# Mixer C's heads emitted in two parts: the second head's projections and convolutions ahead of the first head's later steps

## The chip, the cores and the metric

One core of one Trainium2 chip runs the whole program. The metric is device time in microseconds, the median of three runs; less is better. Engines are named as in the profile: PE is TensorE, PEld its weight loads, DVE VectorE, ACT ScalarE, POOL GpSimd, SP the queue that issues most DMAs.

## What is computed

The reference is a trunk of two layers over 512 tokens of width 1024 in float32. Each layer is a mixer, then 16 experts with top-2 routing, then a gated input embedding. The change is in the second layer's mixer, where mixer C (a gated delta rule, four heads of width 128) and mixer D (forgetting attention, four heads) share one input and one output projection:

```python
def odd_mixer(hn, w_in, w_out, conv_c, a_log, dt_bias, norm_c, fd_bias):
    qc, kc, vc, gc, ac, bc, qd, kd, vd, fd = _split(hn @ w_in, ODD_SPLITS)
    qkv = jax.nn.silu(causal_conv(jnp.concatenate([qc, kc, vc], axis=-1), conv_c))
    ...
    qc = l2norm(_heads(qc, C_HEADS, HEAD_DIM))
    kc = l2norm(_heads(kc, C_HEADS, HEAD_DIM))
    ...
    oc = gated_deltanet(qc, kc, vc, ...)
    out_c = rmsnorm(oc, norm_c) * jax.nn.silu(_heads(gc, C_HEADS, HEAD_DIM))
    ...
    out_d = forgetting_attention(...)
    return jnp.concatenate([_merge(out_c), _merge(out_d)], axis=-1) @ w_out

def gated_deltanet(q, k, v, g, beta):      # per chunk of tokens
    ...
    sol = lax.linalg.triangular_solve(a, rhs, left_side=True, lower=True, unit_diagonal=True)
    ...
    def step(st, xs):                      # over the chunks, one after the other
        v_new = ui - jnp.einsum('bhlk,bhkv->bhlv', wi, st)
        o = jnp.einsum('bhlk,bhkv->bhlv', qdi, st) + jnp.einsum('bhls,bhsv->bhlv', qki, v_new)
        st = cdi[..., None, None] * st + jnp.einsum('bhsk,bhsv->bhkv', kdi, v_new)
        return st, o
```

## The kernel before

Products that need float32 precision are made of three fp32r matmuls (`mm3`, L235 to L237): every operand stands as a high part and a rest. Weights come from memory as 512 KB units, two to a load (`raw`), and `split` makes their two parts: a cast on ACT (L196, `whi`) and a difference on DVE (L197, `wlo`), each in a ring of four buffers. So the split of a unit waits until TensorE has read the unit four places ahead of it.

A head of mixer C is `mixer_c` (L766 to L886). Its **first part**, L767 to L773, makes four projections `proj_f` (q, k, v and the gate `gc`), each 24 matmuls of 512 columns into one PSUM buffer `m` of a pool of four, and a causal convolution with silu on three of them (`conv_silu`, L292 to L302): L294 on ACT evacuates, three L296 on DVE read the same PSUM buffer, L298 on POOL takes a maximum, L299 to L301 on ACT are the sigmoid, L302 on DVE multiplies. The gate is only copied (L773).

Its **later steps** are one chain. Two norms over q and k (`mean_ln`: L336 and L337 on ACT, L338 on DVE, L341 and L342 on TensorE, L344 on ACT), transposes (L795, L800, L815, L823), the inverse of the triangular matrix by six doublings (L828, L833 and the transposes of L837, with L829 and L834 on DVE and L838 on ACT between them), the last of them L842 and L843, the two right-hand sides (L845 to L854), then four chunks one after the other (L858 to L875): L866 makes the output of a chunk, L869 the update, L872 or L874 the new state on DVE, L863 and L864 the next correction. L877 to L886 norm the output, gate it (`e`, from L879 on POOL) and split it into `mixh` and `mixl` for the output projection (`out_proj`, L347).

The chunks here are 128 tokens long, four to the sequence. `mixer_d` (L888) is two projections, logits (L897 to L899), softmax, transposes (L377) and values (L385). `values` makes V for all four heads of mixer D: 96 matmuls into four PSUM buffers of the same pool.

The heads are emitted in the order of this table; tuples are output projections:

```python
ODD_ORDER = ["C0", "C1", "V", "D0", "C2", "D1", "C3", ("C0", "C1"), "D2", ("D0", "C2"), "D3", ("D1", "C3"), ("D2", "D3")]
```

In this stage no order is written out by hand. A scheduler that knows what each instruction waits for takes what is ready, and among that what was emitted first; so a head's chain comes interleaved with the projections that are emitted behind it. Each engine then runs its own list strictly in that order: an instruction that waits holds up all behind it on its engine. The tiles of C0 and C2 come from the ring `c0`, those of C1 and C3 from `c1`, all others of the stage from `w`.

Of the kernel before, what the change touches and what calls it, by code (L numbers as in the profile page):

```python
# [107 lines left out]
def tile_hybrid_trunk(ctx, tc, x, wst, gains, small, lam, rwt, cst, out, stop=None):  # L108
# [33 lines left out]
    class W:  # L142
        psum = turned = None
        banks = {}
        ring = ""
        pos = 0
        next = 0
# [21 lines left out]
    def pm(shape):  # L169
        return W.psum.tile(shape, F32, name="m", bufs=W.banks["m"])  # L170

    def pw(shape):
        n = W.ring if W.ring in W.banks else "w"
        return W.psum.tile(shape, F32, name=n, bufs=W.banks[n])
# [16 lines left out]
    def split(src, a=None, place=None):  # L191

        hi, lo = place or [wp.tile([128, 1024], F32R, name=n) for n in ("whi", "wlo")]
        if place:
            src = src.rearrange("p (k c) -> p k c", c=hi.shape[2])
        nc.scalar.copy(hi, src)  # L196
        nc.vector.tensor_sub(lo, src, hi.bitcast(F32))  # L197
        if a:
            return (hi.rearrange("p (a b) -> p a b", a=a), lo.rearrange("p (a b) -> p a b", a=a))
        return hi, lo  # L200

    def ahead(eng=None, pool=None):

        c = W.next
        if 2 * c >= len(UNITS):
            return
        W.loaded[c] = load(wst[c], eng, pool, c)
        W.next += 1
# [14 lines left out]
    def unit(kind, a=None, place=None):  # L223
        while UNITS[W.pos][0] == "pad":
            W.pos += 1
        assert UNITS[W.pos][0] == kind, (UNITS[W.pos], kind)
        c, half = divmod(W.pos, 2)
        if c not in W.loaded:
            W.next = c
            ahead()  # L230
        W.pos += 1
        return split(W.loaded[c][:, half, :], a, place=place)

    def mm3(ps, l, r, start, stop):
        mm(ps, l[0], r[0], start=start, stop=False)  # L235
        mm(ps, l[0], r[1], start=False, stop=False)  # L236
        mm(ps, l[1], r[0], start=False, stop=stop)  # L237
# [25 lines left out]
    def proj_f(w, parts=1):  # L263
        ps = pm([128, S])
        for i in range(parts):
            c = slice(i * S // parts, (i + 1) * S // parts)
            for k in range(KD):
                mm3(ps[:, c], (w[0][:, k, :], w[1][:, k, :]), (xt[0][:, k, c], xt[1][:, k, c]), k == 0, k == KD - 1)
        return ps
# [13 lines left out]
    def values(v):  # L283


        def emit(t, ps):
            for n in range(NH):
                nc.scalar.copy(v[n][:, t, :HD], ps[:, n * 128:(n + 1) * 128])

        proj_t(emit)  # L290
# [42 lines left out]
    def mean_ln(tmp, src, scale):  # L333

        sq, hi, lo = tmp(), tmp(F32R), tmp(F32R)
        act(sq, src, AF.Square)  # L336
        nc.scalar.copy(hi, sq)  # L337
        tt(lo, sq, hi.bitcast(F32), op=OP.subtract)  # L338
        ps = pw([128, S])
        one = oner.to_broadcast([128, 128])  # L340
        mm(ps, one, hi, start=True, stop=False)  # L341
        mm(ps, one, lo, start=False, stop=True)  # L342
        l = tmp()
        act(l, ps, AF.Ln, bias=epsc, scale=scale)  # L344
        return l

    def out_proj(mix, *halves):  # L347
        m = len(mix)
        for nh in halves or range(2):
            w = [unit("out", 2) for _ in range(m // 2)]  # L350
            for t in range(T):
                c = slice(t * 128, (t + 1) * 128)
                ps = pm([128, 512])
                for j in range(m):
                    x_, w_ = mix[j], w[j // 2]
                    mm3(ps, (x_[0][:, c], x_[1][:, c]), (w_[0][:, j % 2, :], w_[1][:, j % 2, :]), j == 0, j == m - 1)
                r = slice(nh * 512, (nh + 1) * 512)
                tt(h[:, t, r], h[:, t, r], ps, op=OP.add)
# [357 lines left out]
    def odd_mixer():  # L716
        with ExitStack() as cx:
# [46 lines left out]
            mix = {}  # L764

            def mixer_c(o_, n):  # L766
                q, k, v = tmp(), tmp(), tmp()  # L767
                pt = 1 if n else 2
                conv_silu(tmp, proj_f(unit("F", 8), pt), P_CC + 4 * n, q)
# [1 line left out]
                conv_silu(tmp, proj_f(unit("F", 8), pt), P_CC + 4 * (2 * NH + n), v)  # L771
                gc = tmp()
                nc.scalar.copy(gc, proj_f(unit("F", 8)))  # L773
                for src, sc in ((q, HD ** -0.5), (k, 1.0)):
                    l = mean_ln(tmp, src, 1.0)
                    act(l, l, AF.Exp, scale=-0.5)
                    stt(src, src, sc, l, op0=OP.mult, op1=OP.mult)
# [80 lines left out]
                o = pw([128, T, 128])  # L858
# [29 lines left out]
            def mixer_d(o_, n, vd):  # L888
                q, k = tmp(), tmp()
                act(q, proj_f(unit("F", 8)), AF.Copy, scale=HD ** -0.5)  # L890
                nc.scalar.copy(k, proj_f(unit("F", 8)))
                wt = [tmp() for _ in range(T)]

                def logits(i):
                    nk = 128 * (i + 1)
                    ps = pw([128, S])
                    mm(ps[:, :nk], q[:, i * 128:nk], k[:, :nk], start=True, stop=False)  # L897
                    mm(ps[:, :nk], sel[:, n:n + 1].to_broadcast([36, 128]), crs[:, :nk], start=False, stop=False)
                    mm(ps[:, nk - 128:nk], identb, maskq, start=False, stop=True)  # L899
                    return ps  # L900

                ps = logits(0)
                for i in range(T):
                    nk = 128 * (i + 1)
                    p, r = softmax_block(tmp(), ps, nk)
                    if i + 1 < T:
                        ps = logits(i + 1)
                    ts(p[:, :nk], p[:, :nk], r, None, op0=OP.mult)
                    put_Tj(wt, p, i)
                o = pv(vd[n], wt)  # L910
                mix[o_] = finish(xp, o, 5)

            vd = []
            for o in ODD_ORDER:
                W.ring = {"V": "v", "C0": "c0", "C1": "c1", "C2": "c0", "C3": "c1"}.get(o, "w")
                if o == "V":
                    vd = [q3(tmp()) for _ in range(NH)]
                    values(vd)
                elif isinstance(o, tuple):
                    out_proj([mix.pop(n) for n in o])  # L920
                elif o[0] == "C":
                    mixer_c(o, int(o[1]))
                else:
                    mixer_d(o, int(o[1]), vd)

# [575 lines left out]
    with ExitStack() as cx:  # L1501
        layer(0, cx)
        if stop == "ple0":
            return finish_h()
        odd_mixer()
# [124 lines left out]
```

## Time and profile before

| | us |
|---|---|
| median of three runs | 1477.32 (1477.06, 1477.32, 1483.2) |
| the profiled execution, its own time | 1478.86 |
| its span, first to last instruction | 1476.8 |
| TensorE busy | 1392.1 (94%) |
| DVE busy | 1123.4 (76%) |
| ACT busy | 928.6 (63%) |
| POOL busy | 132.4 (9%) |

All rows are of the profiled execution. The odd mixer begins near 699 us, when the last normed tile of the first layer is turned, and ends near 1056, with the last sum into `h`. Busy time of TensorE counts a matmul from its start to its modelled end, and these overlap: the distance from one start to the next tells the pace. The granted clock of the array is given as a share of full speed; it has two levels, 2.4 and 1.2 GHz.

### The profile page before, as it was taken

To read this page: it belongs to the slowest core of one execution; us is meant where nothing else is said; L and a number is where in the kernel's file an instruction comes from. 1 tells how busy PE (TensorE), PEld (TensorE's weight loads), DVE (VectorE), ACT (ScalarE), POOL (GpSimd) and SP (SyncE) were. 2 spreads that over 40 slices of the span, in tenths; PEclk is the share of its full clock that TensorE was granted. 3 is DMA by queue.
4 is the path that set the end of the run, shared out by engine and by line. 5 is a ranking of instruction groups with operands and counts; after the bars stand their busy time and mean duration, and the time that the engine had idled before them with its cause. 6 is when DMAs were issued, how large, how long until landed. Compare 5 with 4: busy or idle time off the path is not lost. (4 is left out here: it accounts for less than half of the span.)

```text
span 1476.8 us, 18718 instructions
## 1 busy us (share of the span) xinstructions
PE 1392.1 (94%) x6812; PEld 1104.7 (75%) x6812; DVE 1123.4 (76%) x1592; ACT 928.6 (63%) x1446; POOL 132.4 (9%) x140
## 2 busy tenths in 40 slices
PE   6999999969999999899989999999879999999796
PEld 4766777758888888667977878786668888888575
DVE  5488557689999999666874666665799999999665
ACT  4256554458888888657464464433458888888545
POOL 2010101010000000030110010000020000000030
PEclk9999999989999999999999999999989999999898
DMA  9223124779999998272411110115589999997261
GB/s 348 89 86 129 61 82 172 255 262 385 408 407 410 403 411 321 94 250 86 145 57 58 58 57 30 58 58 199 187 308 400 406 406 411 406 407 299 74 214 57
DMA packets 54938, 330.62 MB, mean 224 GB/s; under 512 B 6512, under 2 KB 6928, under 8 KB 22320
## 3 DMA queue, kind: packets, MB, share of 16 engines
q1 hardware_dynamic: 36576, 256.67, 44.6%
q0 software_dynamic: 12784, 52.69, 9.8%
q10 hardware_dynamic: 5472, 19.93, 3.4%
q8 instruction: 58, 0.95, 0.3%
q14 instruction: 48, 0.39, 0.1%
HBM read 299.37 MB, written 27.79 MB: 222 GB/s over the span
## 5 line engine op out<-in xcount | busy, mean ns | idle before, releaser
L1269 DVE TENSOR_TENSOR wlo<-raw,whi 128x1024 fp32r<-128x1024 f32 x392 | 456.6, 1219 | 13.8 <-ACT whi L1262 13.7
L1262 ACT CAST whi<-raw 128x1024 fp32r<-128x1024 f32 x392 | 396.0, 1055 | 50.5 <-PE m L237 36.7
L235 PE MATMUL m<-whi,eh 128*128 128x512 f32 x544 | 218.8, 402 | 0.0
L236 PE MATMUL m<-wlo,eh 128*128 128x512 f32 x544 | 215.5, 396 | 0.0
L237 PE MATMUL m<-whi,el 128*128 128x512 f32 x544 | 215.4, 396 | 0.0
L197 DVE TENSOR_TENSOR wlo<-raw,whi 128x1024 fp32r<-128x1024 f32 x110 | 133.3, 1225 | 69.8 <-ACT whi L196 69.5
L196 ACT CAST whi<-raw 128x1024 fp32r<-128x1024 f32 x110 | 113.9, 1050 | 64.6 <-PE m L237 33.3
L235 PE MATMUL m<-xth,whi 128*128 128x512 f32 (+1 forms) x368 | 142.2, 387 | 0.6 <-ACT xth L259 0.5
L237 PE MATMUL m<-xth,wlo 128*128 128x512 f32 (+1 forms) x368 | 141.5, 385 | 0.5 <-DVE wlo L197 0.5
L236 PE MATMUL m<-xtl,whi 128*128 128x512 f32 (+1 forms) x368 | 141.1, 384 | 0.8 <-DVE xtl L260 0.8
L235 PE MATMUL m<-whi,xth 128*128 128x512 f32 x288 | 118.9, 413 | 12.5 <-ACT xth L196 9.1
L237 PEld LDWEIGHTS m<-whi,el 128*128 128x128 f32 x544 | 102.4, 188 | 24.8 <-DVE exf L1112 0.4
L235 PEld LDWEIGHTS m<-whi,eh 128*128 128x128 f32 x544 | 102.7, 189 | 23.4 <-ACT eh L967 0.6
L236 PEld LDWEIGHTS m<-wlo,eh 128*128 128x128 f32 x544 | 102.7, 189 | 23.0
L237 PE MATMUL m<-whi,xtl 128*128 128x512 f32 x288 | 117.3, 408 | 0.5 <-DVE xtl L260 0.3
L236 PE MATMUL m<-wlo,xth 128*128 128x512 f32 x288 | 117.1, 406 | 0.5 <-DVE wlo L197 0.5
L235 PE MATMUL m<-whi,hh 128*128 128x512 f32 x272 | 112.1, 412 | 4.3 <-ACT whi L1262 4.3
L236 PE MATMUL m<-wlo,hh 128*128 128x512 f32 x272 | 109.3, 402 | 1.5 <-DVE wlo L1269 1.5
L237 PE MATMUL m<-whi,hl 128*128 128x512 f32 x272 | 108.8, 400 | 0.0
L237 PEld LDWEIGHTS m<-xth,wlo 128*128 128x128 f32 x368 | 69.7, 189 | 12.9 <-DVE wlo L197 1.0
L236 PEld LDWEIGHTS m<-xtl,whi 128*128 128x128 f32 x368 | 69.7, 189 | 12.5 <-DVE xtl L260 1.0
L235 PEld LDWEIGHTS m<-xth,whi 128*128 128x128 f32 x368 | 69.7, 190 | 12.4 <-ACT xth L259 0.9
(437 smaller groups left out, 2331.7 us busy)
## 6 DMA issues: line engine op xcount, KB each, us to landing
raw<-in_wst_dram SPq DMA_DIRECT2D x238, 1024.0 KB
raw<-in_wst_dram POOLq DMA_DIRECT2D x14, 1024.0 KB, 7.7
yrow<-gbc ACTq DMA_DIRECT2D x16, 512.0 KB
yrow<-y ACTq DMA_DIRECT2D x16, 512.0 KB
xrow<-raw POOLq DMA_DIRECT2D x8, 512.0 KB, 4.3
yrow<-tmp POOLq DMA_DIRECT2D x14, 256.0 KB, 9.5
h<-in_x_dram SPq DMA_DIRECT2D x4, 512.0 KB
raw<-in_wst_dram ACTq DMA_DIRECT2D x2, 1024.0 KB
```

What stands on the lines that cost most here:

```text
L196: nc.scalar.copy(hi, src)
L197: nc.vector.tensor_sub(lo, src, hi.bitcast(F32))
L235: mm(ps, l[0], r[0], start=start, stop=False)
L236: mm(ps, l[0], r[1], start=False, stop=False)
L237: mm(ps, l[1], r[0], start=False, stop=stop)
L1262: nc.scalar.copy(w[0], src)
L1269: nc.vector.tensor_sub(lo, src, hi.bitcast(F32))
```

## The change

`mixer_c` becomes a generator that stops once, behind its first part. For C1 the loop first begins the head (its projections and convolutions) and only then runs C0's later steps and C1's. C2 and C3 run as before, first part and later steps in one go. Nothing is computed otherwise.

```diff
             def mixer_c(o_, n):
+
                 q, k, v = tmp(), tmp(), tmp()
...
                 gc = tmp()
                 nc.scalar.copy(gc, proj_f(unit("F", 8)))
+                yield
                 for src, sc in ((q, HD ** -0.5), (k, 1.0)):
...
-            vd = []
+            vd, begun = [], {}
             for o in ODD_ORDER:
...
                 elif o[0] == "C":
-                    mixer_c(o, int(o[1]))
+                    begun[o] = mixer_c(o, int(o[1]))
+                    next(begun[o])
+
+                    for ring, c in {"C0": (), "C1": (("c0", "C0"), ("c1", "C1"))}.get(o, ((W.ring, o),)):
+                        W.ring = ring
+                        for _ in begun[c]:
+                            pass
```

What it does to the lists of the engines is shown at two places. In the changed program the line numbers from L774 on are one or two higher (L842 is L844, L848 is L850, L863 to L869 are L865 to L871).

**The first norms of C0**, on TensorE. Before, where `m_7889` is C1's k, `m_7929` C1's v, and `c0_7574` the cast square of C0's q:

```order
L237 MATMUL m_7889<-xth_6670,wlo_7886 128x512
L341 MATMUL w_7579<-c0_7574,oner_76 128x512
L235 MATMUL m_7929<-xth_6670,whi_7925 128x512
L236 MATMUL m_7929<-xtl_6671,whi_7925 128x512
L342 MATMUL w_7579<-c0_7575,oner_76 128x512
L237 MATMUL m_7929<-xth_6670,wlo_7926 128x512
```

Now, where `m_7705` is C1's gate, `m_8269` the first of V's four PSUM buffers and `c0_7732` the cast square of C0's q:

```order
L236 MATMUL m_7705<-xtl_6671,whi_7701 128x512
L237 MATMUL m_7705<-xth_6670,wlo_7702 128x512
L341 MATMUL w_7737<-c0_7732,oner_76 128x512
L342 MATMUL w_7737<-c0_7733,oner_76 128x512
L235 MATMUL m_8269<-whi_8273,xth_6670 128x512
```

and a little further on, where `m_8271` is V's third PSUM buffer and `c0_7745` the cast square of C0's k:

```order
L235 MATMUL m_8271<-whi_8273,xth_6670 128x512
L236 MATMUL m_8271<-wlo_8274,xth_6670 128x512
L237 MATMUL m_8271<-whi_8273,xtl_6671 128x512
L235 MATMUL m_8269<-whi_8303,xth_6670 128x512
L341 MATMUL w_7750<-c0_7745,oner_76 128x512
L312 MATMUL w_7757<-brs_7237,sel_75 128x512
L235 MATMUL m_8272<-whi_8273,xth_6670 128x512
L342 MATMUL w_7750<-c0_7746,oner_76 128x512
```

C0's norm of q has moved behind C1's v and gate, and its norm of k into the matmuls of V. On ACT, before, the cast of C0's k (`c0_7587`) stands ahead of the second exponent step of C1's q (`c1_7877`):

```order
L337 CAST c0_7574<-c0_7573 128x512
L196 CAST whi_8303<-raw_8301 128x1024
L299 ACTIVATE c1_7877<-c1_7877 128x512
L344 ACTIVATE c0_7582<-w_7579,epsc_67 128x512
L336 ACTIVATE c0_7586<-c0_7344 128x512
L776 ACTIVATE c0_7582<-c0_7582 128x512
L337 CAST c0_7587<-c0_7586 128x512
L300 ACTIVATE c1_7877<-c1_7877 128x512
```

Now it is `c0_7745`, and stands among the steps of C1's v (`c1_7692`, made from `c1_7687`):

```order
L294 ACTIVATE c1_7687<-m_7662,sm_65 128x512
L196 CAST whi_8361<-raw_8359 128x1024
L344 ACTIVATE c0_7740<-w_7737,epsc_67 128x512
L299 ACTIVATE c1_7692<-c1_7692 128x512
L778 ACTIVATE c0_7740<-c0_7740 128x512
L300 ACTIVATE c1_7692<-c1_7692 128x512
L336 ACTIVATE c0_7744<-c0_7344 128x512
L301 ACTIVATE c1_7692<-c1_7692 128x512
L337 CAST c0_7745<-c0_7744 128x512
L774 COPY c1_7698<-m_7705 128x512
```

It has moved behind the convolutions of C1's q, k and v.

**The last chain, C3's**, on TensorE from its right-hand sides on. Before, where `m_9832` and `m_9864` are D3's projections:

```order
L848 MATMUL w_9470<-c1_9329,c1_9468 128x128 x4
L853 MATMUL w_9477<-c1_9353,c1_9322 128x128 x4
L866 MATMUL w_9485<-c1_9303,c1_9466 128x128
L235 MATMUL m_9832<-xth_6670,whi_9828 128x512
L236 MATMUL m_9832<-xtl_6671,whi_9828 128x512
L237 MATMUL m_9832<-xth_6670,wlo_9829 128x512
L869 MATMUL w_9487<-c1_9466,c1_9483 128x128
```

Now, where `m_9979` belongs to the output projection of D1 and C3, its part for D1:

```order
L237 MATMUL m_9979<-whi_9967,mixl_9109 128x512
L850 MATMUL w_9470<-c1_9329,c1_9468 128x128 x4
L855 MATMUL w_9477<-c1_9353,c1_9322 128x128 x4
L868 MATMUL w_9485<-c1_9303,c1_9466 128x128
L871 MATMUL w_9487<-c1_9466,c1_9483 128x128
L865 MATMUL w_9491<-state_9489,c1_9467 128x128
L867 MATMUL w_9485<-c1_9304,state_9489 128x128
L868 MATMUL w_9485<-c1_9303,c1_9466 128x128
L871 MATMUL w_9496<-c1_9466,c1_9483 128x128
```

The chunk steps now follow each other with nothing between; D3's projections have all moved ahead of them. On DVE at the same place, now:

```order
L845 TENSOR_TENSOR c1_9353<-c1_9353,w_9460 128x512
L197 TENSOR_TENSOR wlo_10080<-raw_10077,whi_10079 128x1024
L847 TENSOR_TENSOR c1_9468<-c1_9353,betc_7235 128x512
L852 TENSOR_TENSOR c1_9353<-c1_9353,ktc_7236 128x512
L858 TENSOR_TENSOR c1_9483<-c1_9322,dc_9298 128x512
```

Before, L843 (now L845) and L845 (now L847) stood side by side; the last weight split of the stage has moved between them.

## Rows read from the trace of the kernel before

**Rows 1.** The page: the span, and the busy time of each engine with its share of the span and its instructions.
```profile
span 1476.8 us, 18718 instructions
PE 1392.1 (94%) x6812; PEld 1104.7 (75%) x6812; DVE 1123.4 (76%) x1592; ACT 928.6 (63%) x1446; POOL 132.4 (9%) x140
```

**Rows 2.** Busy time by stretch of the span: the stretch, its length, busy us and instructions of PE, PEld, DVE, ACT and POOL, the granted clock, the DMA engines' share and GB/s.
```profile
700.00:750.00 50.00, 44.78 (x289) 40.01 (x290) 39.73 (x57) 27.22 (x47) 8.90 (x5) 0.98 0.38 128
740.00:750.00 10.00, 5.35 (x21) 3.98 (x20) 7.60 (x11) 6.09 (x10) 3.82 (x2) 0.92 0.32 106
750.00:800.00 50.00, 49.41 (x293) 40.73 (x292) 29.90 (x53) 23.36 (x39) 2.98 (x2) 0.98 0.12 43
1000.00:1050.00 50.00, 48.38 (x222) 34.34 (x222) 25.44 (x53) 17.80 (x51) 3.65 (x5) 0.97 0.49 192
```

**Rows 3.** What TensorE waited for between 690 and 1040 us: who, whom, us in total, times, the longest.
```profile
PE w L341 <- ACT c L337: 4.6, 1, 4.6
...
PE w L377 <- DVE w L908: 1.6, 1, 1.6
```

**Rows 4.** TensorE in order of time around the wait in front: start, duration, line, output and inputs, and in brackets the idle time before it and what ended it.
```profile
743.16 0.40 PE L236 MATMUL m<-xtl,whi 128*128 128x512 f32 x1
743.39 0.39 PE L237 MATMUL m<-xth,wlo 128*128 128x512 f32 x1
748.43 0.80 PE L341 MATMUL w<-c,oner 128*128 128x512 f32 x1 [4.65 <-ACT c L337]
749.02 0.63 PE L235 MATMUL m<-xth,whi 128*128 128x512 f32 x1
749.45 0.63 PE L236 MATMUL m<-xtl,whi 128*128 128x512 f32 x1
...
753.79 0.40 PE L341 MATMUL w<-c,oner 128*128 128x512 f32 x1
...
758.38 0.60 PE L795 MATMUL w<-cs,c 128*128 128x128 f32 x4
```

**Rows 5.** ACT in order of time in the same place: the first sigmoid steps of C0's k and v, the copy of C0's gate and the cast of C0's q.
```profile
737.35 0.63 ACT L299 ACTIVATE c<-c 128x512 f32<-128x512 f32 x1 [3.90 <-POOL c L298]
...
744.77 0.63 ACT L299 ACTIVATE c<-c 128x512 f32<-128x512 f32 x1 [3.36 <-POOL c L298]
...
746.63 0.57 ACT L773 COPY c<-m 128x512 f32<-128x512 f32 x1
...
747.76 0.62 ACT L337 CAST c<-c 128x512 fp32r<-128x512 f32 x1
```

**Rows 6.** DVE in order of time in the same place: the three L296 of C0's v and a weight split.
```profile
739.95 2.31 DVE L296 SCALAR_TENSOR_TENSOR c<-m,sm,c 128x511 f32<-128x511 f32 x3
742.17 1.22 DVE L197 TENSOR_TENSOR wlo<-raw,whi 128x1024 fp32r<-128x1024 f32 x1
```

**Rows 7.** POOL in order of time: the maxima of C0's k and v and of C1's q, and L879 of C0.
```profile
734.99 2.33 POOL L298 TENSOR_SCALAR c<-c 128x512 f32<-128x512 f32 x1 [5.17 <-DVE c L296]
742.40 2.33 POOL L298 TENSOR_SCALAR c<-c 128x512 f32<-128x512 f32 x1 [5.09 <-ACT c L294]
748.26 1.49 POOL L298 TENSOR_SCALAR c<-c 128x512 f32<-128x512 f32 x1 [3.52 <-DVE c L296]
...
803.25 1.72 POOL L879 TENSOR_SCALAR c<-c 128x512 f32<-128x512 f32 x1 [28.41 <-PE w L869]
```

**Rows 8.** TensorE in order of time at the end of the stage, from L842 of C3 to the output projection of D1 and C3; the matmul at 1021.25 is the first that reads C3's result.
```profile
997.29 1.13 PE L842 MATMUL w<-c,c 128*128 128x128 f32 x8
...
1000.08 1.13 PE L848 MATMUL w<-c,c 128*128 128x128 f32 x8
...
1001.94 0.43 PE L866 MATMUL w<-c,c 128*128 128x128 f32 x2
...
1002.91 0.38 PE L869 MATMUL w<-c,c 128*128 128x128 f32 x2
...
1003.84 0.40 PE L863 MATMUL w<-state,c 128*128 128x128 f32 x2
...
1004.75 0.38 PE L866 MATMUL w<-c,c 128*128 128x128 f32 x2
1004.97 0.39 PE L869 MATMUL w<-c,c 128*128 128x128 f32 x2
...
1009.68 0.38 PE L866 MATMUL w<-c,c 128*128 128x128 f32 x2
...
1019.58 0.41 PE L377 MATMUL w<-cs,w 128*128 128x128 f32 x2 [1.57 <-DVE w L908]
...
1021.25 0.58 PE L235 MATMUL m<-whi,mixh 128*128 128x512 f32 x1
1021.62 0.63 PE L236 MATMUL m<-wlo,mixh 128*128 128x512 f32 x1
1022.05 0.63 PE L237 MATMUL m<-whi,mixl 128*128 128x512 f32 x1
```

**Rows 9.** DVE in order of time in the same place.
```profile
1003.34 0.29 DVE L874 COPY state<-w 128x128 f32<-128x128 f32 x1 [2.07 <-PE w L869]
1004.27 0.29 DVE L864 TENSOR_TENSOR c<-c,w 128x128 f32<-128x128 f32 x1 [0.64 <-PE w L863]
...
1016.16 1.23 DVE L197 TENSOR_TENSOR wlo<-raw,whi 128x1024 fp32r<-128x1024 f32 x1 [0.53 <-ACT whi L196]
```

**Rows 10.** ACT in the same place: the cast of the stage's last weight unit.
```profile
1015.09 1.05 ACT L196 CAST whi<-raw 128x1024 fp32r<-128x1024 f32 x1 [0.17 <-PE m L236]
```

## Prediction

> **What bounds the kernel now.** I read the page's busy shares first, then the busy time by stretch, then the list of who TensorE waits for, then the order of time on the four engines at two places. The page says TensorE works for 94% of the span [rows 1]. In the odd mixer, where the change is, the stretches say the same more sharply: 49.41 of 50 us at 750 to 800, against 44.78 at 700 to 750 and 48.38 at 1000 to 1050 [rows 2]. So the stage is a queue of TensorE work with few holes, and a change of order can only fill holes or make new ones. What can be filled is small: the list of waits has one of 4.6 us on the ACT cast of L337 and one of 1.6 us on the DVE scaling of L908 [rows 3], and the rest sums to less than these. Each hole costs a little more than itself, because the array comes back at half pace: main matmuls start every 0.23 us before the large wait and every 0.43 us after it [rows 4], and the matmul durations stretch to 0.63 us after the small one too [rows 8]. The granted clock is 0.92 at 740 to 750, and 0.97 over the last 50 us [rows 2].
>
> **What the order says.** All work is the same; 16 projections, 4 chains of head steps and the fillers between them stand in another order. I call a 512-column matmul of a projection a main matmul. In front, between the wait and the first transposes of C0 (L795), TensorE had 29 main matmuls before and has 81 now: all of C1's v and gate, then 33 of V. At the end, between L842 of C3 and the first matmul that reads C3's result (an output projection), it had 46 main matmuls before and has 7 now. Everything between is the same chain on other cover, with four to seven main matmuls behind each step as before; I cost it at nothing, and the cover is V and D0's q and k for C0, C2's projections for C1, and so on. POOL's and SP's queues hold the same instructions, POOL with C1's three maxima (L298) ahead of C0's L879, before which POOL stood idle for 28.41 us anyway [rows 7], and with four weight loads ahead of C3's L879; these wait for D3's last projection, which now ends before C3's steps do. I cost both at nothing.
>
> **The front.** The wait of 4.65 us goes: C1's v and gate need no result that is late (their weights were split, and their PSUM buffers come free with L296 of C0's v at 739.95 + 2.31 [rows 6] and the copy L773 at 746.63 + 0.57 [rows 5]). What is late next are the convolutions. ACT, DVE and POOL work on one convolution at a time: ACT's L299 of C0's k, at 737.35, and of v, at 744.77, are 7.42 us apart [rows 5], since the next evacuation L294 stands behind L301 in ACT's queue; inside lie 2.31 us of L296 on DVE [rows 6] and 2.33 us on POOL [rows 7]. A projection on TensorE takes 24 x 0.23 = 5.5 us. With six convolutions in a row TensorE gains 1.9 us on each and runs out of the four PSUM buffers. The POOL maximum of C1's q starts at 748.26 and takes 1.49 [rows 7]; nothing ahead of it has moved, so C1's q has its L299 at 749.8, k at 757.2, v at 764.6. C1's v gives its PSUM buffer back when POOL can start on it, at about 764.6 - 2.33 - 0.1 = 762.1. TensorE reaches the V matmuls that need this buffer (m_8271) at 743.6 + 48 x 0.23 + 0.7 for L341 and L342 + 12 x 0.23 = 758.1: **a new wait of 4 us**. The next one is L341 of C0's k. Its cast L337 stood ahead of C1's L300 on ACT and stands now behind C1's v, the sixth ACT instruction from 764.6; at a pitch of 0.6 (L773 to L337 is two in 1.13) it starts 3.0 later, and with its 0.62 [rows 5] it ends at 768.2, while TensorE is there at 762.1 + 7 x 0.23 = 763.7: **another 4.5 us**. From L341 of k to L795 it took 758.38 - 753.79 = 4.6 [rows 4], so L795 comes at 772.8, 14.4 later than before, with 52 more main matmuls done (52 x 0.23 = 12.0). The front loses 2.4 us instead of gaining 6.
>
> What the trace does not show is POOL's time for C1's k and v. The rows have 2.33 where DVE's split (L197) starts just ahead of it, as at 742.17 and 742.40 [rows 6, 7], and 1.49 elsewhere. The new order puts a split behind both, so I take 2.33; at 1.49 twice the front loses 0.7. The upper bound is the slow pace after both waits: the first wait cost some 7 matmuls x 0.2 = 1.4 us on top [rows 4], so +3.8. The Trainium skill ("SBUF — State Buffer", section "Who interferes with whom") holds that VectorE and GpSimd take one shared port pair as an exclusive lock, so that the later one blocks fully. Here the split would hold POOL until 743.39, which makes 0.99 + 1.49 = 2.48 where the row has 2.33; for the two together the lock would add 0.3 us to the front's loss, and no lock would take off 1.7. The measured 2.33 decides; it lies near the lock.
>
> **The end.** The chain of C3 took 1021.25 - 997.29 = 23.96 us from L842 to the first matmul on its result [rows 8]; the cover is now gone, so I add the chain up. L842 to L848 is 2.79 [rows 8]; a weight split stands now between L843 and L845 on DVE, 1.2 us more (1.22 for one [rows 6]): 4.0. L848 to the first L866 is 1.9 [rows 8]. Then three chunk updates: L869 to DVE's copy 0.43 and 0.29 for it, L863 to L864 0.43 and 0.29 again [rows 8, 9], two hand-overs of 0.1 (DVE's end at 1003.63 to L863 at 1003.84 is the upper bound of one) and 0.2 from L866 to L869 [rows 8], 1.9 each, 5.6 in all, where they took 1009.68 - 1001.94 = 7.74 between main matmuls [rows 8]. From the last L866 to the output projection it was 11.57 [rows 8]; the weight split that lay in it, L196 on ACT ahead of L883 and L197 on DVE ahead of L884 [rows 9, 10], is gone, about 1.0, so 10.6. Sum 22.1 us. TensorE's own load in it falls by 39 x 0.23 = 9.0 and gains 0.3 of transposes. Had the old order lost nothing more, 23.96 - 9.0 + 0.3 = 15.3 would do; **the end loses 22.1 - 15.3 = 6.8 us**, as waits of L848, of the nine update matmuls and of the output projection. Bounds: without the split in the way and with 1.5 us saved by an emptier DVE, +4; with the array at half pace through the stretch (a matmul takes 0.63 us for 0.40 then [rows 4, 8], and some 13 of them stand one behind the other in this chain), 3 us more, +10. I take the sum, because its durations are of the same instructions.
>
> **Sum.** +2.4 + 6.8 = +9.2 us. The profiled execution took 1478.86 us, of which 1476.8 is span; it would become 1488.1. It is 1.5 above the median of the three runs, 1477.32, so I forecast 1486.5. What follows the stage (routing, experts) starts from the end of the odd mixer and is passed on unchanged.
>
> **Rivals.**
> - *The front pays.* If the convolutions keep TensorE's pace once no head steps lie between them, the wait of 4.65 and 1.4 of slow pace go, -6; with the end's +6.8 that is 1478. For it: DVE is busy for 29.90 and ACT for 23.36 of the 50 us from 750 [rows 2]. Against it: the 7.42 us were measured where no head steps lay between. Chance 0.20.
> - *Slow clock.* The end is idle for 6.8 of 22.1 us in pieces of 1 to 2 us. One piece of 1.57 was followed by a slow stretch at 1021 [rows 8]. With 3 us more at the end, by the bound above, and 1.4 behind each of the front's waits it is +6: 1492.5. Against it: at 1002 to 1009 the steps ran at full pace. Chance 0.14.
> - *Faster.* C3's chain is shorter than I add up, because nothing else stands in DVE's and ACT's queues. It decides at 15.3 us from L842 to the output projection: below, the end costs nothing and its old wait (1.57, and 1.5 of slow pace) goes too. With the front's -6 that makes 1468. Against it: 2.79 + 1.9 + 10.6 is 15.3 already, without one chunk update. Chance 0.05.
> - *Forecast*, both waits: 0.61.
>
> **How the numbers follow.** About 0.5% (7.4 us) is what a measurement of this kernel can tell from no change. Slower by more: four fifths of the forecast's cases (its own range is 1482 to 1491, and a fifth of it lies under 1484.7) and the slow clock, 0.62. Faster: 0.05. The rest, 0.33. The range reaches from the first rival to above the second, 1478 to 1494, and leaves out the faster one and the thin ends.
>
> **What would show it.** Right: L341's wait on C0's q gone; a TensorE wait of 3 to 4 us of a V matmul on DVE's L296 and one as long of L341 on ACT's L337, both at 758 to 769; L795 near 773; L842 of C3 to the output projection 21 to 23 us with holes at L848 and between the chunk updates; the stage ending some 9 us later. Wrong in front: L795 before 769. Wrong at the end: less than 17 us, or other main matmuls between the updates than the order shows.

## The result

The changed kernel takes 1496.97 us (1496.71 to 1499.27, four runs) against 1479.08 (1477.06 to 1483.2, four runs) for the kernel before on the same chip: a ratio of 1.0124, 95% interval 1.0111 to 1.0137. It is **slower by 17.9 us**; the forecast was 9.2 slower, and the range ended 3 us below the result. The direction and both places were right, the sizes were not.

From here on, L797 of the changed kernel is L795 of before, L844 is L842, and so on (two lines more from L775).

The page of the changed kernel, first lines, and its busy time by stretch (columns as in [rows 2]):

```profile
span 1494.9 us, 18719 instructions
PE 1401.2 (94%) x6812; PEld 1109.9 (74%) x6812; DVE 1125.9 (75%) x1592; ACT 928.8 (62%) x1446; POOL 132.2 (9%) x140
```
```profile
700.00:750.00 50.00, 48.18 (x305) 43.28 (x306) 41.13 (x59) 28.62 (x50) 6.58 (x4) 0.97 0.37 128
740.00:750.00 10.00, 10.00 (x45) 8.06 (x44) 6.52 (x9) 6.59 (x12) 2.33 (x1) 1.00 0.29 105
750.00:800.00 50.00, 44.57 (x228) 35.47 (x227) 27.83 (x46) 24.20 (x42) 6.14 (x3) 0.93 0.12 43
1000.00:1050.00 50.00, 43.04 (x213) 30.30 (x212) 21.92 (x44) 15.82 (x38) 3.63 (x5) 0.86 0.37 147
```

The hole of 740 to 750 is gone. Against [rows 2], TensorE's busy time falls from 49.41 to 44.57 at 750 to 800 and from 48.38 to 43.04 at 1000 to 1050, and the granted clock with it. The same is in the list of who TensorE waits for in the changed kernel, from 690 to 1110 (in all, times, longest):

```profile
PE w L341 <- ACT c L337: 5.1, 2, 3.8
...
PE w L377 <- DVE w L910: 2.2, 2, 1.2
...
PE m L235 <- DVE c L296: 1.7, 1, 1.7
...
PE w L839 <- DVE c L836: 1.1, 2, 0.6
PE w L850 <- DVE c L847: 1.1, 1, 1.1
```

**Where the 18 us lie.** The first main matmul of C0's q and the last matmul of the last output projection bound the stage, before and now:

```profile
698.72 0.62 PE L235 MATMUL m<-xth,whi 128*128 128x256 f32 x3 [0.46 <-ACT xth L259]
...
1054.61 0.39 PE L237 MATMUL m<-whi,mixl 128*128 128x512 f32 x1
```
```profile
701.65 0.62 PE L235 MATMUL m<-xth,whi 128*128 128x256 f32 x3 [0.46 <-ACT xth L259]
...
1073.37 0.40 PE L237 MATMUL m<-whi,mixl 128*128 128x512 f32 x1
```

The stage takes 371.7 us instead of 355.9: **15.8 of the 18.1 us** between the two spans. 2.9 arose ahead of it and 0.6 was given back behind it, in parts that the change does not touch. Ten of the eleven kernels below start the stage between 699.1 and 700.6 (the other one alters the stages ahead), so part of that 2.9 is how two executions differ; the rest was not followed.

To see where inside the stage, I take an account of TensorE: each of its instructions at a fixed weight (0.233 us for 512 columns of a main matmul, 0.12 for 256, 0.15 for a step of 128, 0.2 to 0.235 for longer ones), summed in program order. The sum is 302.6 us for every kernel here. What a stretch took beyond its sum is called lost in it. Example: before, the first transposes come 758.38 - 698.72 = 59.7 us into the stage with 50.8 of work ahead of them: 8.9 lost. "Left" is the main matmuls, at full pace, behind C3's last doubling (L842 before).

The weights of the steps are low: the four products of L842 take 0.88 us at full clock (997.29 to 998.17), 0.22 each. With the distances of the full-pace rows instead, the work is 326.8 us, and before has 10.1, 12.7 and 6.2 lost, the change 13.8, 14.5 and 16.6. So much of a column, the middle one above all, is work and not loss; the differences between kernels are what the table tells, and those come out the same (3.7, 1.8 and 10.4).

| kernel | time | ahead of C0's first transposes | up to C3's last doubling | from there to the end | left |
|---|---|---|---|---|---|
| before | 1479 | 8.9 | 31.8 | 12.6 | 31.6 |
| change | 1497.0 | 12.5 | 33.6 | 23.0 | 22.6 |
| e1_yield_k | 1479.2 | 9.1 | 32.4 | 11.2 | 31.6 |
| e2_yield_v | 1488.0 | 10.7 | 32.9 | 18.0 | 26.3 |
| e3_fill_end | 1491.9 | 12.5 | 33.6 | 9.9, fillers counted as work | 22.6 + 11.2 |
| e4_five_banks | 1503.2 | 12.4 | 32.8 | 21.6 | 22.6 |
| e5_pair_steps | 1482.8 | 12.6 | 34.5 | 9.5 | 37.2 |
| e6_both_pairs | 1486.0 | 16.2 | 29.4 | 16.2, a longer stretch | 56.5 |
| e7_max_on_dve | 1483.1 | 4.0 | 29.3 | 21.7 | 22.6 |
| e8_before_max_on_dve | 1478.4 | 4.1 | 28.5 | 19.2 | 26.3 |
| e9_norm_first | 1492.5 | 7.6 | 32.1 | 23.3 | 23.0 |
| e10_pair_and_max | 1468.3 | 4.3 | 28.8 | 10.2 | 33.5 |
| e11_pairs_and_max | 1466.3 | 4.2 | 23.3 | 14.5, a longer stretch | 56.5 |

The change costs 3.6 us in front (forecast 2.4), 1.8 between (forecast nothing) and 10.4 at the end (forecast 6.8). Each line is one execution, and two executions differ: behind L842 e1 has TensorE's order of before, instruction by instruction, and loses 11.2 there for 12.6. One difference in front is not the order's either. In the changed kernel and in nine of the eleven others TensorE runs at half pace for some 3 us near 725 (granted clock 0.57 at 724 to 728 in the changed kernel, 1.00 at 722 to 726 before) and loses 1.5, in projections ahead of all that the change moves; the executions of before, e4 and e6 do not have it there. Where TensorE waits further on in the front, it comes to that wait later and waits less; where no wait is left (e7, e8, e10, e11), the 1.5 is part of the 4.0 to 4.3.

**The front, as forecast.** TensorE and ACT of the changed kernel in order of time:

```profile
764.38 0.47 PE L235 MATMUL m<-whi,xth 128*128 128x512 f32 x1 [1.67 <-DVE c L296]
...
765.86 0.40 PE L235 MATMUL m<-whi,xth 128*128 128x512 f32 x1
770.02 0.79 PE L341 MATMUL w<-c,oner 128*128 128x512 f32 x1 [3.76 <-ACT c L337]
...
771.46 0.79 PE L235 MATMUL m<-whi,xth 128*128 128x512 f32 x1
...
777.00 0.60 PE L797 MATMUL w<-cs,c 128*128 128x128 f32 x4
```
```profile
751.89 0.63 ACT L299 ACTIVATE c<-c 128x512 f32<-128x512 f32 x1 [0.45 <-POOL c L298]
...
759.33 0.63 ACT L299 ACTIVATE c<-c 128x512 f32<-128x512 f32 x1 [3.95 <-POOL c L298]
...
766.75 0.63 ACT L299 ACTIVATE c<-c 128x512 f32<-128x512 f32 x1 [3.37 <-POOL c L298]
...
769.36 0.60 ACT L337 CAST c<-c 128x512 fp32r<-128x512 f32 x1
```

C1's three L299 stand 7.44 and 7.42 us apart, the cycle that the forecast took from C0's [rows 5]. Both waits are there: V's matmul for its PSUM buffer, 1.7 us (forecast 4; 1.5 of the difference is the half pace near 725, by which TensorE came later), and L341 for the cast L337, 3.8 (forecast 4.5). Behind the second main matmuls have 0.63 to 0.79 us and start every 0.43 for 4 us, which I had left to the upper bound; behind the first they keep full pace.

**The end.** TensorE from C3's last doubling to the first matmul that reads C3's result:

```profile
1014.67 1.13 PE L844 MATMUL w<-c,c 128*128 128x128 f32 x8
1018.49 1.13 PE L850 MATMUL w<-c,c 128*128 128x128 f32 x8 [1.05 <-DVE c L847]
...
1020.34 0.43 PE L868 MATMUL w<-c,c 128*128 128x128 f32 x2
...
1026.36 0.49 PE L868 MATMUL w<-c,c 128*128 128x128 f32 x2 [0.16 <-DVE c L866]
1028.18 0.69 PE L341 MATMUL w<-c,oner 128*128 128x512 f32 x1 [1.33 <-ACT c L337]
...
1033.28 1.49 PE L899 MATMUL w<-w 128*128 128x384 f32 x2
...
1036.80 0.66 PE L377 MATMUL w<-cs,w 128*128 128x128 f32 x2 [1.20 <-DVE w L910]
...
1040.40 0.78 PE L235 MATMUL m<-whi,mixh 128*128 128x512 f32 x1
```

From L844 it is 3.8, 1.9, 6.0 and 14.0 us to these marks; forecast 4.0, 1.9, 5.6 and 10.6. Only the last is off. The granted clock by stretch, in the changed kernel:

```profile
1020.00:1025.00 5.00, 3.77 (x25) 2.89 (x23) 1.22 (x4) 0.82 (x2) 0.00 (x0) 1.00 1.01 426
1025.00:1030.00 5.00, 3.07 (x13) 2.20 (x13) 1.37 (x4) 1.21 (x2) 1.48 (x1) 0.83 1.00 424
1030.00:1035.00 5.00, 4.00 (x9) 1.77 (x8) 1.63 (x5) 3.43 (x9) 0.00 (x0) 0.50 0.64 269
1035.00:1040.00 5.00, 3.80 (x9) 1.40 (x9) 2.92 (x7) 1.51 (x5) 0.00 (x0) 0.50 0.00 0
```

At 1030 to 1040 TensorE runs at 0.50, that is 1.2 GHz, and what it runs there is D3: logits (L899 to L901) and transposes (L377). The two last heads share every queue. ACT and DVE show how D3's pace becomes C3's:

```profile
1034.14 0.63 ACT L885 ACTIVATE c<-c 128x512 f32<-128x512 f32 x1
```
```profile
1035.63 0.56 DVE L363 TENSOR_REDUCE nm<-w 128x1 f32<-128x384 f32 x1 [2.14 <-PE w L901]
...
1036.57 0.75 DVE L886 SCALAR_TENSOR_TENSOR c<-w,sm,c 128x512 f32<-128x512 f32 x1
```

C3's L886 reads what L885 made by 1034.77, but stands in DVE's queue behind D3's row maximum, which waited 2.14 us for logits that TensorE made at half pace, and starts at 1036.57.

### The profile page after: what moved, and what is told of

Its sections match the earlier page's. It is cut to its first block, busy times and chain, and to the rows that moved or that the text cites. A ratio compares the mean times of both kernels' runs of the same rounds, so it can differ in the third digit from the quotient of the medians.

```text
span 1494.9 us, 18719 instructions
## 1 busy us (share of the span) xinstructions
PE 1401.2 (94%) x6812; PEld 1109.9 (74%) x6812; DVE 1125.9 (75%) x1592; ACT 928.8 (62%) x1446; POOL 132.2 (9%) x140
## 5 line engine op out<-in xcount | busy, mean ns | idle before, releaser
L196 ACT CAST whi<-raw 128x1024 fp32r<-128x1024 f32 x110 | 114.1, 1050 | 69.3 <-PE m L237 33.3
L237 PEld LDWEIGHTS m<-xth,wlo 128*128 128x128 f32 x368 | 70.3, 191 | 12.5 <-DVE wlo L197 1.0
```

## The experiments

Theory A: the chains of the four heads stand one behind the other, and every us of projections that runs ahead of the first is cover that the last one lacks; its holes then also bring the clock down. Rival B: the waits in front are the loss. Rival C: at the end it is the chain's latency alone, not the clock.

**Dose.** The second head stops earlier.

```diff
                 conv_silu(... P_CC + 4 * (NH + n), k)
+                if n == 1:
+                    yield
...
-                yield
+                if n != 1:
+                    yield
```

> The second head stops after its k convolution; its v and gate are emitted behind the first head's later steps. In the order of the instructions TensorE then has main matmuls worth 48.3 us at full pace ahead of the first head's first transposes (46.4 before the change, 58.5 with it), and from the first head's L842 on the order is that of the kernel before. Theory A, borrowed cover (each us of matmuls put ahead of the first head's chain is missing under the last head's chain): 1477 to 1480, the end of the stage as before (24 us from the third line of the update chain, L842, to the first output projection on the last head's result), a wait of 2 to 3 us left in front. Rival B, the early start itself disturbs the front (convolutions and head steps in each other's way): 1482 to 1486, with new waits at the first head's norms.

Measured: 1479.23 us, ratio 0.9999 (0.9988 to 1.0010). The order behind the last head is that of before, and its loss, 11.2 us, is near that of before (12.6). In front the wait of L341 on L337 is 3.4 us (4.6 before; TensorE came to it 1.5 later, by the half pace near 725), and 0.2 us more is lost than before.

The same with the two lines behind v's convolution:

> The second head stops after its v convolution; only its gate is emitted behind the first head's later steps. Main matmuls ahead of the first head's transposes: 53.2 us (46.4 before, 58.5 with the whole change). Main matmuls left behind the last head's L842: 26.3 us (31.6 before, 22.6 with the change). Theory A, borrowed cover: about 0.55 of the loss of the whole change, 1487 to 1490. Rival B, the loss is that of the six convolutions in a row in front and of the waits they cause: nearly the whole loss, 1494 to 1497.

Measured: 1487.99 us, ratio 1.0061 (1.0041 to 1.0080), half of the loss, as A had it and B had not: the front lost 1.8 us more than before, the end 5.4.

**Fillers at the end**, behind D3 in the changed kernel:

```diff
+                if o == "D3":
+                    for i in range(48):
+                        ps = pm([128, S])
+                        mm(ps, xt[0][:, i % KD, :128], xt[0][:, i % KD, :], start=True, stop=True)
```

> The whole change, and 48 matmuls of 512 columns that nobody reads (11.2 us at full pace) at the lowest place in the order, which puts 11 behind L844 of the last head, 2 to 3 between its chunk updates, 6 behind the last update and 13 between the last softmax head's steps. They do no useful work; they only fill holes. Theory A with the clock (the holes let the array fall to half pace, and the last heads' steps at half pace are part of the loss): granted clock 1.0 from 1015 to 1045, L844 to the output projection 21 to 23 us instead of 25.7, the time 2 to 4 us shorter, 1493 to 1495. Rival C, the chain's latency alone is the loss: no gain, or up to 2 us more where a filler stands in the way, 1497 to 1499.

Measured: 1491.94 us (1491.47 to 1493.87), 5.0 less than the changed kernel and 1 below what A with the clock expected, with 11 us more on TensorE. Its stretches:

```profile
1025.00:1030.00 5.00, 5.00 (x26) 3.51 (x24) 1.46 (x4) 1.72 (x3) 1.43 (x1) 1.00 0.00 0
1030.00:1035.00 5.00, 5.00 (x21) 2.74 (x20) 3.16 (x8) 3.30 (x12) 0.00 (x0) 1.00 0.00 0
1035.00:1040.00 5.00, 5.00 (x22) 3.50 (x22) 3.12 (x7) 2.28 (x8) 2.16 (x4) 1.00 0.26 64
```

The clock is 1.00 throughout. From L844 to the last L868 the fillers cost time, 13.3 us for 11.7; from there to the matmul on C3's result it is 11.3 for 14.0, 2.7 less. The cast L408 makes C3's result; with fillers and in the changed kernel it stands at

```profile
1035.81 0.62 ACT L408 CAST mixh<-c 128x512 fp32r<-128x512 f32 x1 [0.28 <-DVE c L887]
```
```profile
1038.38 0.63 ACT L408 CAST mixh<-c 128x512 fp32r<-128x512 f32 x1
```

and ends 10.1 and 12.7 us behind the last L868: 2.6 less at full clock, although fillers share TensorE's queue. That puts the price of the half pace there at 2.6 or more. Together 24.6 us, more than the 21 to 23 expected. So C is wrong about the clock and right about the larger part: the chain takes some 24 us with 46 main matmuls under it (23.96 before), with 48 fillers (24.6) and with next to nothing (25.7). What the change lost at the end is mainly the useful work that stood there. The profiled execution is the slowest of its four runs; it is 1.8 us shorter than that of the change in the stage and begins the stage 1.6 earlier, which the fillers do not touch. So 1.8 is what the stage shows; why the medians differ by 5.0 stays open.

**A fifth PSUM buffer** for the projections, three for the head steps:

```diff
-    banks(ctx, m=4, w=4)
+    banks(ctx, m=5, w=3)
```

> The whole change with five PSUM buffers for projections and three for the head steps (four and four before). The wait of a V matmul for its PSUM buffer on L296 (1.8 us) goes. Theory A: the first head's cast L337 is as late as it was, its wait grows by what the other one gave, and the time stays within 1.5 us, 1495.5 to 1498.5. Rival B, each wait in front is a loss of its own: 1.8 us and some slow pace less, 1493 to 1495. With three buffers the head steps could also get in each other's way; that would show as waits of their first matmuls and 1500 or more.

Measured: 1503.2 us (1500.08 to 1504.84). This missed both theories on the total. The total is that of the third way (three buffers hold the head steps up, 1500 or more), but it does not arise in this stage, which is 2.3 us shorter than with the change: the other stages have the three buffers too, the odd mixer begins 5.4 us later than with the change, and behind it 1.8 more pass. In the stage's front 12.4 us are lost instead of 12.5, with this list from 707 to 790:

```profile
PE w L341 <- ACT c L337: 5.2, 1, 5.2
PE m L235 <- DVE c L296: 1.8, 1, 1.8
```

V's wait is still there with five buffers, so the run does not show what its absence is worth and decides nothing between A and B; L341's is longer than the 3.8 of the change.

**More cover at the end**, with the front as it is. A `yield` ahead of each group of steps lets the loop run C0 and C1 in turn:

```diff
-                    for ring, c in {...}.get(o, ((W.ring, o),)):
-                        W.ring = ring
-                        for _ in begun[c]:
-                            pass
+                    live = [(r, begun[c]) for r, c in {...}.get(o, ((W.ring, o),))]
+                    while live:
+                        for e in list(live):
+                            W.ring = e[0]
+                            if next(e[1], 1):
+                                live.remove(e)
```

> The whole change, and the later steps of the first two heads emitted in turn (one step of C0, one of C1) instead of one head after the other; C2 and C3 as before. Main matmuls ahead of the first head's first transposes: 62.5 us at full pace (46.4 before, 58.5 with the change); behind the last head's L842: 37.2 us (31.6 and 22.6). Theory A, the four heads' chains stand one behind the other and what decides is how much TensorE work is left when the last one runs: the end is covered again and the time comes back to 1477 to 1483, though the first head starts later than in any kernel so far. Rival B, the loss is paid in front, with each us of projections ahead of the first head: 1497 to 1502.

Measured: 1482.79 us, ratio to before 1.0028 (1.0015 to 1.0040). The first transposes come 21 us later than before and the end loses 9.5 us, less than before. B would have had 1497 or more. C2 and C3 in turn as well (`"C2"` only begun, C3 ahead of D1 in the table):

> As the run with the first pair in turn, and C2 and C3 in turn as well, C3's projections ahead of D1's. Main matmuls behind the last head's L842: 56.5 us. Theory A: no hole under the last head, the granted clock 1.0 to the end of the stage, 1472 to 1480; what is left over the full pace is the front. Rival B: 1497 to 1502. A third way, the two heads' steps in each other's way on DVE and ACT, would show as many waits of TensorE of 0.5 to 1 us inside the pair and 1482 to 1490.

Measured: 1485.96 us, ratio 1.0047 (1.0030 to 1.0064); A's number was 1480 at most. No wait is left under the last head, but six convolutions in a row now stand at two places, and from 890 to 960 TensorE's list has

```profile
PE w L341 <- ACT c L337: 4.9, 1, 4.9
```

So the third way was right in size and wrong in place: the price is the convolutions', not the pair's steps'.

**The front.** The maximum of L298 on DVE for the heads of this mixer, in the changed kernel and in the kernel before:

```diff
-        nc.gpsimd.tensor_scalar(e, acc, -80.0, None, op0=OP.max)
+        (nc.vector if W.ring in ("c0", "c1") else nc.gpsimd).tensor_scalar(e, acc, -80.0, None, op0=OP.max)
```

> The whole change, with the maximum of L298 of this mixer's heads on DVE instead of POOL. It shortens the cycle of one convolution over ACT, DVE and POOL (7.4 us), which I hold for the cause of the two waits in front. Main matmuls ahead of the first transposes 59.2 us, behind the last head's L844 22.6, as with the change. Theory A with that cause: the convolutions come 5.5 to 6 us apart, the wait of L341 on L337 falls from 3.8 us to under 1.5 and the V matmul's wait goes, the first head's L797 comes 3 to 5 us earlier and the end keeps its holes: 1492 to 1494.5. If the cause is the order on ACT alone (L337 behind the last convolution): 1496 to 1498.

Measured: 1483.14 us, 14 less than the changed kernel, four times what I expected. The front loses 4.0 us, both waits are gone, and between 4.3 less is lost. The end loses 21.7 with its 22.6 left. But the convolutions did not come closer: L299 of C1's k and v are 8.0 us apart. What moved is the order: on ACT, L337 of C0's k now stands ahead of C1's last L299.

> The kernel before, with the maximum of L298 of this mixer's heads on DVE instead of POOL. The heads' order is that of before, but the program's order puts 52.7 us of main matmuls ahead of the first head's first transposes (46.4 before) and leaves 26.3 behind the last head's L842 (31.6 before, 26.3 in the run where the second head stopped after v). Theory A: the wait of 4.65 us in front goes (5 to 6 us with its slow pace), and the end loses some 5 us for it: 1477 to 1482. Rival B, the front decides: 1471 to 1475.

Measured: 1478.35 us, ratio 0.9999 (0.9989 to 1.0008), A's number: 4.8 won in front, 3.3 between, 6.6 lost at the end, where the cover fell to 26.3.

To part POOL's time from ACT's order, the maximum stays on POOL and only the first head's norms come earlier in the order:

```diff
-                for src, sc in ((q, HD ** -0.5), (k, 1.0)):
-                    ...
+                with tc.high_priority(offset=60 if n == 0 else 0):
+                    for src, sc in ((q, HD ** -0.5), (k, 1.0)):
+                        ...
```

> The whole change, with the first head's two norms (L776 to L779 and what they call) given a higher place in the order; the maximum stays on POOL. On ACT the cast L337 of the first head's k now stands ahead of L299 of the second head's k and v (behind both before). Main matmuls ahead of the first transposes: 50.8 us instead of 58.5; behind the last head's L844: 23.0, as with the change (22.6). If the front's loss comes from the place of L337 on ACT, the waits on L337 and on the V matmul's buffer fall under 2 us together, TensorE's loss up to the first transposes is 5 to 8 us instead of 12.5, the end loses 22 to 23 us as with the change, and the time is 1489 to 1493. If it comes from POOL's 2.33 us inside each convolution, the V matmul waits as long and the time is 1495 to 1498.

Measured: 1492.5 us (1491.23 to 1497.05), as expected of ACT's order. ACT of this kernel:

```profile
750.81 0.63 ACT L299 ACTIVATE c<-c 128x512 f32<-128x512 f32 x1 [0.46 <-POOL c L298]
...
754.85 0.62 ACT L337 CAST c<-c 128x512 fp32r<-128x512 f32 x1
...
766.01 0.63 ACT L299 ACTIVATE c<-c 128x512 f32<-128x512 f32 x1 [1.36 <-POOL c L298]
```

L337 of C0's k comes 14.5 us earlier than in the changed kernel and nothing waits for it; 1.3 us are left on the cast of C0's q, and V's wait is gone. The front loses 7.6, less than before the change, and still the kernel is 14 us slower than before: that is the end, 23.3, with 23.0 left. B falls. Of the 8.5 us that the maximum on DVE won in front, the earlier norms alone give 4.9, and of its 4.3 between 1.5; the rest is not separated.

**Both cures together.**

> The first two heads' later steps emitted in turn and the maximum of L298 on DVE: the end's cover (as in the run of the pair alone, where the end lost 9.5 us where the kernel before lost 12.6) and the front without its waits (as in the run of the maximum alone, where TensorE had lost 4.0 us at the first transposes instead of 12.5). Main matmuls behind the last head's L842: 33.5 us (31.6 before). If the two add up: 1482.8 - 8.5 = 1474, 1471 to 1477, faster than the kernel before. If front and end pay for each other whatever the order: 1477 to 1481.

Measured: 1468.31 us, ratio 0.9933 (0.9918 to 0.9947). C0 and C1 in turn and the maximum on DVE: 4.3 lost in front, 10.2 at the end, and 28.8 between, where the pair alone lost 34.5; with that it is under the range expected.

> Both pairs of heads in turn and the maximum on DVE. Main matmuls behind the last head's L842: 56.5 us. The second pair's convolutions stand in a row too and waited in the run without the maximum on DVE; they should not now. If both fronts lose 8 us less: 1486 - 16 = 1470, 1467 to 1475. If the steps of two heads hold each other up on DVE and ACT: 1476 to 1482.

Measured: **1466.25 us, ratio 0.9913 (0.9899 to 0.9928)**, the fastest, 0.75 under the range expected. Its page and two stretches:

```profile
span 1465.0 us, 18696 instructions
PE 1389.4 (95%) x6812; PEld 1108.5 (76%) x6812; DVE 1129.4 (77%) x1604; ACT 926.8 (63%) x1446; POOL 109.1 (7%) x128
```
```profile
750.00:800.00 50.00, 49.94 (x291) 41.91 (x290) 35.34 (x69) 30.68 (x62) 0.00 (x0) 1.00 0.19 65
1000.00:1050.00 50.00, 49.73 (x235) 35.72 (x234) 27.08 (x51) 20.90 (x63) 2.91 (x6) 1.00 0.62 237
```

TensorE is full at both places that the change had emptied, at full clock.

## Why the prediction was wrong in size

- **The end's last term is the step that failed**: "the weight split that lay in it ... is gone, about 1.0, so 10.6". It took 14.0, because without main matmuls between, D3's steps stand next in the same queues, the clock falls to 0.50 as they begin, and C3's steps wait behind D3's on DVE. I had the half pace as a bound of 3 us and as a rival of 0.14, and left it out of the sum; it came. What I held against it, the full pace of the steps at 1002 to 1009, is true of C3's chunk steps in the change too (1.00 to 1028) and says nothing of D3's steps behind them. L844 to the output projection was 25.7 for 22.1, the end's loss 25.7 - 15.3 = 10.4 for 6.8, just above the upper bound of 10. I had the chain get shorter without its cover (22.1 for 23.96); it got longer. The half pace is at least 2.6 us of that by the run with fillers. This term is 3.4 of the 6.6 us by which the stage was mis-sized (15.8 for 9.2).
- **"Everything between ... I cost it at nothing"** was 1.8 us. The list has small waits on the doublings in C1 (L839 on L836, 1.1). It was not tested by itself and stays open, as do the 4.3 us that the maximum on DVE won there; the kernels lie between 28.5 and 34.5 in that stretch.
- **The front** was right in mechanism (both waits, the 7.4 us cycle, the cast behind C1's v) and 1.2 us short: 3.6, just under its upper bound of 3.8. L341 of k came 1.1 us earlier in the stage than forecast (770.02 - 701.65 = 68.4 for 768.2 - 698.72 = 69.5), but from it to the first transposes it took 7.0 for 4.6, at the slow pace that I had left to the bound. The two waits together were 3.0 us shorter than forecast; this slow pace and the 1.5 us near 725, which the execution before does not have, stand in their place.
- **What I did not see is the link**, though it is not what made the number wrong. I priced front and end as two places. The table shows one quantity: the less is left behind the last doubling, the more the end loses, whatever the front does. 31.6 left cost 11.2 and 12.6, 26.3 cost 18.0 and 19.2, 22.6 to 23.0 cost 21.6 to 23.3: about 1.2 us for each us of cover taken, with a spread of 1 to 2 us between kernels that have the same left, and little to gain above some 33 (10.2 at 33.5, 9.5 at 37.2).
- Of the rivals, the front that pays was wrong by the same two waits; "slow clock" described the end, at 1492.5, and was still 4.5 short, some 2 of which lie outside the stage; in front the clock fell behind one of the two waits, not behind both.

## What to carry to other kernels

Where a long chain with no work of its own at the end of a stage lives on independent work that the order puts under it, count that work as a stock: whatever is pulled ahead of the first link is missing under the last, at the end's price and clock, not at the pace of the work moved. Before a chain's cover is used elsewhere, shorten the row of chains (two heads in turn instead of one behind the other) and look in each in-order queue for the one cast that all others wait for. When the holes come, the array is at half pace for whatever stands next, so price that too.

## What the runs showed of the hardware

- POOL needs 1.49 us for the maximum of L298 over 128 x 512 float32, and 2.33 where a weight split on DVE has just begun (756.73 and 756.96 in the changed kernel); DVE needs 0.42:

```profile
756.96 2.33 POOL L298 TENSOR_SCALAR c<-c 128x512 f32<-128x512 f32 x1 [5.10 <-issue]
```
```profile
737.23 0.42 DVE L298 TENSOR_SCALAR c<-c 128x512 f32<-128x512 f32 x1
```

  The Trainium skill ("GPSIMD Engine Reference", section "4.1 Engine selection") calls one-input elementwise work on GpSimd roughly line-rate; these rows, 3.5 times apart without a neighbour, say otherwise. The Trainium skill ("Perfetto Trace Analysis", section "Optimizing Scalar/DVE Operations") warns that moving work between GpSimd and DVE might not help, since they share a read port; here the move was worth 14 us with the change and nothing without it. 4.5 of the 14 came with the earlier norms alone (1492.5); the rest was not separated.
- In the changed kernel the granted clock stayed at 1.00 from 1018 to 1028, through holes of TensorE of 0.16 to 1.05 us, and was down to 1.2 GHz (0.69 us for L341 where 0.40 is usual) behind the hole of 1.33 before 1028.18, 0.58 on average from 1028 to 1030; it stayed at 0.50 from 1030 to 1040 while TensorE was busy for 3.8 to 4.0 of each 5 us.
